# Opening of a hybrid decoder trunk: constant products on TensorE ahead of the first transposes, another order of the first weight loads, and a row load on another queue

## The chip, the core and the metric

The kernel runs on one core of one Trainium2 chip. The core has TensorE (matrix products and transposes into PSUM; its weight loads stand in the profile as PEld), VectorE (DVE), ScalarE (ACT), GpSimd (POOL) and SyncE (SP), which here only issues DMAs. ScalarE and GpSimd issue DMAs too, each on a queue of its own. The metric is the device time of one execution in microseconds; the kernel before and the kernel after are compared by the medians of their runs.

## The reference

One layer over 1024 rows of 1024 channels. A condition vector c makes a shift, a scale and a gate by a product with a 1024 x 3072 matrix; x is normalised, scaled and shifted to h; h goes through one combined input projection; two linear-attention branches run on the projections; they are merged, projected, added to x and normalised. The change lies in the first steps:

```python
c_act = jax.nn.silu(c)
mod = c_act @ ada_w[l] + ada_b[l]
shift, scale, gate = jnp.split(mod, 3, axis=-1)
h = rms_norm(x, norm_w[l]) * (1.0 + scale[:, None, :]) + shift[:, None, :]
proj = h @ w_in[l]
hq, hf, hi, hz, gq, gk, gv, gz, ga, mg = jnp.split(proj, IN_OFFSETS, axis=-1)
```

All inputs are f32. What follows behind the projection (the two attention branches, the gates, the output projection, the final norm) is the same before and after.

## The kernel before

**Numbers.** Products are made in the fp32r form. Each f32 operand is split in two: ScalarE rounds it to a high part (`split`, line 196) and VectorE subtracts that to get the rest, the low part (line 197). A product then is three: high by high, high by low, low by high.

**The opening**, up to `order.close()`, computes h for the first 512 rows and, while h is being made, the first 768 columns of the projection (six blocks of 128, `NG = 6`), for those 512 rows. h is made transposed, in eight tiles d = 0 to 7 of 128 channels. For each d four 128 x 128 blocks of x are transposed on TensorE (`turn_x`, line 219) into a PSUM tile, which ScalarE copies out (`copy_x`, line 224); `make_h` scales and shifts it on ScalarE by that tile's modulation (line 233) and splits it. Then `products(d, ns)` (line 352) adds the 18 products of this d, six for each of the three kinds in `ns`: 0 needs the high parts alone, 1 the low part of h, 2 the low part of the weights.

**Modulation blocks.** Shift and scale come in five blocks, `blocks = [(0, 1), (1, 2), (3, 2), (5, 2), (7, 1)]`, each (first d, number of d). `load_mod(bi)` (line 251) fetches a block's columns: four DMAs of 256 KB for a block of one d, eight for a block of two. `add_mod` (lines 265 and 267, VectorE) sums the first half of the 1024 rows, weighted by c; `mm_mod` (line 277, TensorE) sums the second half as four small f32 matmuls; `end_mod` adds the two (line 283, VectorE), sums over the partitions on TensorE (line 287, the "column sums") and adds the bias (lines 290 and 292).

**Weight tiles.** `load_wg(k)` (line 315) fetches the 768 weight columns of rows 128k to 128k + 127, 384 KB. Tiles 0 to 2 and 5 to 7 share three places, so tile 5, 6 or 7 can be loaded only when tile 0, 1 or 2 has been split. `prep_wg(k)` splits one: two roundings on ScalarE, two subtractions on VectorE.

**Order.** In the opening the order on TensorE, ScalarE and VectorE is that of the program text (`manual_schedule`). DMAs go out in the order of the text on the engine that issues them. Nearly all loads are SyncE's: c, four tiles of x (512 KB each), then block 0, weight tile 0, tiles 1 and 2, block 1, tiles 3 and 4, block 2, and later tiles 5 and 6, block 3, tile 7, block 4 and the second half of x. ScalarE's queue loads `rows_a` (ada_b and norm_w, 24 rows that `vec_rows` transposes on TensorE at line 154); GpSimd loads `rows_b` and the small gate weights. A square, a root, a reciprocal and a product per x tile (lines 203 to 210) normalise x ahead of the transposes.

In the text, behind `load_mod` and `load_wg`, come the squares and scales of x, `vec_rows(rows_a)`, the transposes of d = 0, the sums of block 0, and then a loop over the blocks: make h for this block's d, split the next block's weight tiles, sum the next block's modulation, and between these steps the products. `products` of a d stand around `mm_mod` and `end_mod` of the next block, so that TensorE has work while VectorE sums.

Behind `order.close()` the framework's scheduler sets the order of the instructions on the engines, by times that it models, within the data's dependences. The rest of the kernel (line 541 and on: projections, attention, merging, the products of line 1343, the output stage of line 1520) is ordered so.

Of the kernel before, what the change touches and what calls it, by code (L numbers as in the profile page):

```python
# [9 lines left out]
F32 = mybir.dt.float32  # L10
# [73 lines left out]
def hybrid_trunk_kernel(  # L84
# [6 lines left out]
    nc = tc.nc  # L91
# [17 lines left out]
    def mtile():  # L109
        cnt[0] += 1  # L110
        return ps_m.tile([P, 512], F32, tag="m", name=f"pm{cnt[0]}")

    sc_ps = ps_s.tile([P, T], F32, name="sc_ps")


    ident = cp.tile([P, P], F32, name="ident")
    make_identity(nc, ident)
    ones = cp.tile([P, P], F32, name="ones")
# [11 lines left out]
    rows_c = cp.tile([8, P], F32, name="rows_c")  # L130
    rows_a = cp.tile([24, P], F32, name="rows_a")
# [3 lines left out]
    def row_load(eng, dst, src):  # L135
        eng.dma_start(dst, src.rearrange("(r p) -> r p", p=P))

    def load_x(t):
        b = S.get([D])
        nc.sync.dma_start(b, x2[t * P:(t + 1) * P, :])  # L140
        return b

    row_load(nc.sync, rows_c, c[0])
    x_t = [load_x(t) for t in range(4)]
    row_load(nc.scalar, rows_a[0:16, :], ada_b[0, 0:2 * D])
    row_load(nc.scalar, rows_a[16:24, :], norm_w[0])
    row_load(nc.gpsimd, rows_b[0:8, :], lb_logits[0])
    row_load(nc.gpsimd, rows_b[8:16, :], hgrn_norm_w[0])
    row_load(nc.gpsimd, rows_b[16:20, :], alpha_b[0])
# [2 lines left out]
    def vec_rows(rows, n, at):  # L152
        pv = mtile()
        i = nc.tensor.transpose(pv[:, 0:n], rows, ident[0:n, 0:n])
        nc.vector.tensor_copy(vec[:, at:at + n], pv[:, 0:n])
        return i
# [34 lines left out]
    def split(src, hi=None, lo=None):  # L191

        if hi is None:
            hi = S.get(list(src.shape[1:]), F32R)
            lo = S.get(list(src.shape[1:]), F32R)
        nc.scalar.copy(hi, src)  # L196
        nc.vector.tensor_sub(lo, src, hi.bitcast(F32))  # L197
        return hi, lo
# [8 lines left out]
    def scale_x(t, xt):  # L207
        r = rsx[:, t:t + 1]
        nc.vector.reciprocal(r, r)
        nc.vector.tensor_scalar_mul(xt, xt, r)  # L210

    turned = {}

    def turn_x(half, xs, d):
        if d % 2 == 0:
            hT[half, d // 2] = S.get([2, 512])
        turned[half, d] = mtile()
        for i in range(4):
            nc.tensor.transpose(turned[half, d][:, i * P:(i + 1) * P], xs[i][:, d * P:(d + 1) * P], ident)
        if d == KT - 1:  # L220
            S.free(*xs)

    def copy_x(half, d):
        nc.scalar.copy(hT[half, d // 2][:, d % 2, :], turned.pop((half, d)))

    def transpose_x(half, xs, d):
        turn_x(half, xs, d)
        copy_x(half, d)
# [14 lines left out]
    def load_mod(bi):  # L243
        d0, nd = blocks[bi]
        kq = 4 // nd
        mods[bi] = []
        for kk in range(KT // kq):
            b = S.get([kq, 2, nd * P])
            for half in range(2):
                c0 = half * D + d0 * P  # L250
                nc.sync.dma_start(b[:, :, half, :], ada_w[0, kk * kq * P:(kk + 1) * kq * P, c0:c0 + nd * P].rearrange(
                    "(k p) f -> p k f", p=P))
            mods[bi].append(b)

    def mod_acc(bi):
        nd = blocks[bi][1]
        return scT_f[:, bi % 2 * 512:bi % 2 * 512 + 2 * nd * P].rearrange("p (a f) -> p a f", a=2)
# [13 lines left out]
    def mm_mod(bi):  # L271
        kq = 4 // blocks[bi][1]
        w = 2 * blocks[bi][1] * P
        mod_ps[bi] = mtile()
        for j in range(4):
            k = 4 + j
            nc.tensor.matmul(mod_ps[bi][32 * j:32 * j + 32, 0:w], cs32[:, k, :],
                             mods[bi][k // kq][:, k % kq].rearrange("p a f -> p (a f)"), start=True, stop=True)

    def end_mod(bi):  # L280
        d0, nd = blocks[bi]
        acc = mod_acc(bi)
        nc.vector.tensor_add(acc, acc, mod_ps.pop(bi)[:, 0:2 * nd * P].rearrange("p (a f) -> p a f", a=2))
        pm = mtile()
        for half in range(2):
            for i in range(nd):
                nc.tensor.matmul(pm[:, half * nd + i:half * nd + i + 1], acc[:, half, i * P:(i + 1) * P], one_t,
                                 start=True, stop=True)
        S.free(*mods.pop(bi))
        nc.vector.tensor_add(modv[:, :, d0:d0 + nd], pm[:, 0:2 * nd].rearrange("p (a b) -> p a b", a=2),  # L290
                             vec[:, R_SH:R_SH + 16].rearrange("p (a b) -> p a b", a=2)[:, :, d0:d0 + nd])
        nc.vector.scalar_tensor_tensor(amul[:, d0:d0 + nd], modv[:, 1, d0:d0 + nd], 1.0,
                                       vec[:, R_NW + d0:R_NW + d0 + nd], ALU.add, ALU.mult)
# [3 lines left out]
    wa_hi = [S.get([2, 512], F32R) for _ in range(4)]  # L297
    wa_lo = [S.get([2, 512], F32R) for _ in range(4)]
    wb_hi = [S.get([4, 256], F32R) for _ in range(2)]
    wb_lo = [S.get([4, 256], F32R) for _ in range(2)]  # L300
# [7 lines left out]
    raws = {}  # L308

    def load_wg(k):  # L310
        if k in (3, 4):
            raws[k] = S.get([T])
        else:
            raws[k] = xb_f[:, (k % 5 % 3) * 768:(k % 5 % 3) * 768 + 768]
        nc.sync.dma_start(raws[k][:, 0:NG * P], w_in[0, k * P:(k + 1) * P, C_GQ:C_GQ + NG * P])

    def prep_wg(k):
        raw = raws.pop(k)
        split(raw[:, 0:512], wa_hi[k // 2][:, k % 2, :], wa_lo[k // 2][:, k % 2, :])
        split(raw[:, 512:768], wb_hi[k // 4][:, k % 4, :], wb_lo[k // 4][:, k % 4, :])  # L320
        if k in (3, 4):
            S.free(raw)

    g_state = {}
    wga = cp.tile([P, KT, 16], F32, name="wga")
# [24 lines left out]
    def product(half, d, f, n):  # L350
        a, b = ((0, h_hi), (0, h_lo), (1, h_hi))[n]
        nc.tensor.matmul(accs[f], wg(a, d, f), b[d][:, half * 512:half * 512 + 512],  # L352
                         start=(d == 0 and n == 0), stop=(d == KT - 1 and n == 2))

    def products(d, ns):
        for n in ns:
            for f in range(NG):
                product(0, d, f, n)

    load_mod(0)  # L360
    load_wg(0)
    load_wg(1)
    load_wg(2)
    load_mod(1)
    load_wg(3)
    load_wg(4)
    load_mod(2)
# [1 line left out]
        square_x(i, x_t[i])  # L369
        scale_x(i, x_t[i])  # L370
    vec_rows(rows_a, 24, R_SH)
    transpose_x(0, x_t, 0)
    add_mod(0)
    mm_mod(0)
    end_mod(0)
    prep_wg(0)
    x_t2 = []
    for bi, (d0, nd) in enumerate(blocks):
        ds = range(d0, d0 + nd)
        more = bi + 1 < len(blocks)  # L380
        nxt = range(blocks[bi + 1][0], sum(blocks[bi + 1])) if more else ()
        for d in ds:
            make_h(0, d)
            if (0, d + 2) in turned:
                copy_x(0, d + 2)
        if not more:
            break
        for d in nxt:
            prep_wg(d)
        add_mod(bi + 1)  # L390
        if nd == 1:
            for d in nxt:
                transpose_x(0, x_t, d)
            products(d0, (0,))
            mm_mod(bi + 1)
            products(d0, (1,))
            end_mod(bi + 1)
            products(d0, (2,))
            turn_x(0, x_t, nxt[-1] + 1)
        else:  # L400
            late = x_t2 if bi == 3 else ()
            for i, xt in enumerate(late[:2]):
                square_x(4 + i, xt)
                scale_x(4 + i, xt)
            products(d0, (0, 1))
            if bi > 1:
                transpose_x(0, x_t, nxt[0])
            for i, xt in enumerate(late[2:]):
                square_x(6 + i, xt)
            mm_mod(bi + 1)  # L410
            products(d0, (2,))
            for d in nxt[1:]:
                transpose_x(0, x_t, d)
            products(d0 + 1, (0,))
            end_mod(bi + 1)
            for i, xt in enumerate(late[2:]):
                scale_x(6 + i, xt)
            products(d0 + 1, (1, 2))
        if bi == 0:
            load_wg(5)  # L420
            load_wg(6)
            load_mod(3)
            load_wg(7)
            load_mod(4)
        elif bi == 1:
            x_t2.extend(load_x(t) for t in range(4, 8))
    products(KT - 1, (0,))
# [119 lines left out]
    class Feat:  # L547

        raws, parts = 1, 2
# [16 lines left out]
    class Vblk:  # L566

        raws, parts = 2, 4
# [41 lines left out]
    class Vblk2:  # L610

        raws, parts = 4, 8
# [400 lines left out]
    class First:  # L1013
        raws, parts = 0, 0
# [435 lines left out]
    for g in BUILT[1:]:  # L1450
        n = GROUPS.index(g)
# [201 lines left out]
    for b in (2, 3):  # L1653
        for p, i, z in ((3, 3, "11"), (6, 1, "21"), (6, 3, "12"), (7, 2, "22")):
            after(b - 1, p, i, lambda b=b, z=z: load_quad(b, z))
            if b == 3:
                p, i = {(3, 3): (7, 2), (6, 1): (7, 3), (6, 3): (4, 2), (7, 2): (4, 3)}[p, i]
# [61 lines left out]
```

## Time and profile before

| What | Value |
|---|---|
| Median of 3 runs | 1216.99 us (1215.41 to 1218.84) |
| Profiled execution, its own time | 1216.46 us |
| Its span, first to last instruction | 1214.8 us |
| Mean granted TensorE clock | 0.998 |
| TensorE busy | 1184.1 us, 97% of the span |
| VectorE, ScalarE, GpSimd busy | 65%, 45%, 10% |
| Moved by DMA | 183.51 MB, mean 151 GB/s |

In the rows of the profile, `PE L352 MATMUL pd<-b,b 128*128 128x512 f32 x4` is four matmuls of line 352 on TensorE, into the PSUM tile pd, with a 128 x 128 stationary and a 128 x 512 moving operand. A timeline row begins with its start and its duration in microseconds; a bracket at its end gives how long the engine stood idle before it and what ended that. The fp32r type of the operands of line 352 stands as f32 there. A row of windows has the stretch, its length, the busy time of PE, PEld, DVE, ACT and POOL, the granted clock, the share of the DMA engines, and GB/s. Rows of DMA issues end with the size of each and the time from issue to landing. Matmuls overlap in the pipeline, so the duration of one is longer than the distance to the next.

### The profile page before, as it was taken

To read this page: it belongs to the slowest core of one execution; us is meant where nothing else is said; L and a number is where in the kernel's file an instruction comes from. 1 tells how busy PE (TensorE), PEld (TensorE's weight loads), DVE (VectorE), ACT (ScalarE), POOL (GpSimd) and SP (SyncE) were. 2 spreads that over 40 slices of the span, in tenths; PEclk is the share of its full clock that TensorE was granted. 3 is DMA by queue.
4 is the path that set the end of the run, shared out by engine and by line. 5 is a ranking of instruction groups with operands and counts; after the bars stand their busy time and mean duration, and the time that the engine had idled before them with its cause. 6 is when DMAs were issued, how large, how long until landed. Compare 5 with 4: busy or idle time off the path is not lost.

```text
span 1214.8 us, 20860 instructions
## 1 busy us (share of the span) xinstructions
PE 1184.1 (97%) x8579; PEld 982.6 (81%) x8579; DVE 790.9 (65%) x1245; ACT 546.9 (45%) x797; POOL 123.8 (10%) x215
## 2 busy tenths in 40 slices
PE   5999999999999999999999999999999999999997
PEld 3777889889798888888887888877778888878886
DVE  4637444774848456877884365794653775988994
ACT  5646732434434244344332324455743544444554
POOL 4100000202111121121110101011220000000000
PEclk9999999999999999999999999999999999999999
DMA  9814000844444267255341112054697746435523
GB/s 320 277 70 139 18 19 19 293 141 161 156 152 149 66 207 249 94 179 169 108 174 47 59 53 70 36 174 158 227 343 277 260 160 208 135 104 173 174 104 122
DMA packets 130961, 183.51 MB, mean 151 GB/s; under 512 B 7467, under 2 KB 97633, under 8 KB 130866
## 3 DMA queue, kind: packets, MB, share of 16 engines
q1 hardware_dynamic: 117250, 136.87, 35.7%
q0 software_dynamic: 13568, 45.31, 9.6%
q8 instruction: 67, 1.10, 0.4%
q14 instruction: 28, 0.23, 0.1%
q10 hardware_dynamic: 48, 0.01, 0.0%
HBM read 132.87 MB, written 49.28 MB: 150 GB/s over the span
## 4 chain that ended last, share of the span: by engine, by line
PE 61%; issue 23%; DVE 3%; ACT 3%; POOL 2%; DMA 1%; POOLq 0%; ACTq 0%; DVEq 0%
PE pd L541 19%; PE pd L1343 9%; PE sc_ps L1343 5%; PE pm L1343 5%; PE pd L1520 3%; PE pd L643 2%; PE pd L644 2%; PE pd L645 2%; PE sc_ps L1520 2%; PE pm L848 1%; PE pd L352 1%; PE pm L829 1%; PE pm L850 1%; PE pm L1520 1%; PE sc_ps L352 1%
## 5 line engine op out<-in xcount | busy, mean ns | idle before, releaser
L541 PE MATMUL pd<-b,b 128*128 128x512 f32 x1632 | 387.4, 394 | 0.0
L541 PEld LDWEIGHTS pd<-b,b 128*128 128x128 f32 x1632 | 302.4, 188 | 64.8 <-issue 1.4
L1343 PE MATMUL pd<-b,b 128*128 128x512 f32 x720 | 173.7, 392 | 4.3 <-ACT b L1414 2.1
L1343 PEld LDWEIGHTS pd<-b,b 128*128 128x128 f32 x720 | 133.7, 188 | 35.7 <-ACT b L1414 3.2
L197 DVE TENSOR_TENSOR b<-b,b 128x1024 fp32r<-128x1024 f32 (+2 forms) x89 | 98.9, 1122 | 83.1 <-ACT b L196 65.4
L196 ACT CAST b<-b 128x1024 fp32r<-128x1024 f32 (+2 forms) x89 | 82.9, 948 | 92.1 <-DVE b L1199 14.6
L1286 DVE TENSOR_TENSOR b<-b,b 128x1024 fp32r<-128x1024 f32 x56 | 68.3, 1224 | 66.9 <-ACT b L1285 52.3
L1285 ACT CAST b<-b 128x1024 fp32r<-128x1024 f32 x56 | 58.3, 1050 | 73.9 <-PE pd L1343 20.6
L1343 PE MATMUL sc_ps<-b,b 128*128 128x512 f32 x324 | 79.4, 391 | 1.0 <-ACT scT L793 1.0
L600 PE MATMUL pd<-b,b 128*128 128x256 f32 x256 | 74.2, 290 | 0.0
L1264 DVE TENSOR_TENSOR b<-b,b 128x1024 fp32r<-128x1024 f32 x48 | 59.2, 1251 | 20.8 <-ACT b L1263 15.1
L602 PE MATMUL pd<-b,b 128*128 128x256 f32 x256 | 72.5, 283 | 0.0
L601 PE MATMUL pd<-b,b 128*128 128x256 f32 x256 | 72.4, 283 | 0.0
L1343 PEld LDWEIGHTS sc_ps<-b,b 128*128 128x128 f32 x324 | 60.3, 188 | 14.6 <-ACT scT L793 1.4
L1343 PE MATMUL pm<-b,b 128*128 128x512 f32 x300 | 72.1, 389 | 0.0
L1263 ACT CAST b<-b 128x1024 fp32r<-128x1024 f32 x48 | 49.9, 1050 | 41.2 <-PE pd L1343 16.0
L1343 PEld LDWEIGHTS pm<-b,b 128*128 128x128 f32 x300 | 56.3, 188 | 11.7
L352 PE MATMUL pd<-b,b 128*128 128x512 f32 x192 | 53.3, 410 | 2.0 <-ACT b L196 0.9
L1201 POOL DMA_DIRECT2D ws<-b x64 | 34.6, 541 | 192.0 <-DVE b L1195 86.5
L735 ACT COPY xb<-b 128x512 f32<-128x512 f32 x48 | 29.4, 620 | 49.4 <-PE sc_ps L715 26.7
L643 PE MATMUL pd<-b,b 128*128 128x512 f32 x128 | 51.3, 401 | 0.0
L644 PE MATMUL pd<-b,b 128*128 128x512 f32 x128 | 50.0, 390 | 0.0
(285 smaller groups left out, 1964.3 us busy)
## 6 DMA issues: line engine op xcount, KB each, us to landing
b<-in_w_in_dram SPq DMA_DIRECT2D x66, 512.0 KB, 4.2
ws<-b POOLq DMA_DIRECT2D x64, 256.0 KB, 3.3
b<-ws SPq DMA_DIRECT2D x32, 512.0 KB, 4.9
b<-in_x_dram SPq DMA_DIRECT2D x16, 512.0 KB, 5.7
b<-in_ada_w_dram SPq DMA_DIRECT2D x32, 256.0 KB, 6.9
b<-in_w_branch_dram SPq DMA_DIRECT2D x16, 512.0 KB, 4.4
b<-h SPq DMA_DIRECT2D x14, 512.0 KB, 4.3
wo<-b POOLq DMA_DIRECT2D x14, 512.0 KB, 5.7
```

Of the source, the lines that this page charges most:

```text
L196: nc.scalar.copy(hi, src)
L197: nc.vector.tensor_sub(lo, src, hi.bitcast(F32))
L352: nc.tensor.matmul(accs[f], wg(a, d, f), b[d][:, half * 512:half * 512 + 512], start=(d == 0 and n == 0), stop=(d == KT - 1 and n == 2))
L541: nc.tensor.matmul(ps[0:w, th * 512:(th + 1) * 512], a[:, k, 0:w], b[:, th * 512:(th + 1) * 512], start=(k == 0 and n == 0), stop=(k == KT ...
L600: nc.tensor.matmul(o, lh, hi[:, k % 4, :], start=(k == 0), stop=False)
L601: nc.tensor.matmul(o, lh, lo[:, k % 4, :], start=False, stop=False)
L602: nc.tensor.matmul(o, ll, hi[:, k % 4, :], start=False, stop=(k == KT - 1))
L643: nc.tensor.matmul(o, lh, hi[:, k % 2, :], start=(k == 0), stop=False)
L644: nc.tensor.matmul(o, lh, lo[:, k % 2, :], start=False, stop=False)
L1286: nc.vector.tensor_sub(lo, t, hi.bitcast(F32))
L1343: nc.tensor.matmul(o, a[:, sl], c, start=(p in (1, 5) and kt == 0 and n == 0), stop=(kt == 3 and n == 2), skip_group_check=True)
L1520: nc.tensor.matmul(o, a, b, start=(p in (1, 5) and kt == 0 and n == 0), stop=(kt == 3 and n == 2), skip_group_check=True)
```

## The change

Six edits, all in the opening.

- c is loaded by ScalarE's queue instead of SyncE's, and norm_w by GpSimd's instead of ScalarE's.
- `keep_busy(n)` multiplies two constant 128 x 128 f32 tiles (ones and the identity) n times, into columns of `sc_ps` that the first products overwrite later. Seven stand ahead of the transposes of d = 0; one, three, one and two stand behind the first to the fourth of these transposes; one stands behind `mm_mod(0)`; two stand ahead of the first products.
- Block 1 of the modulation is loaded ahead of weight tiles 1 and 2.
- The split of a weight tile is cut in two functions, `prep_hi` (ScalarE) and `prep_lo` (VectorE).
- Tiles 1 and 2 are no longer split ahead of block 1's sum. Tile 1 is rounded behind that sum, and its subtraction and the split of tile 2 stand between the two h tiles of block 1.
- The loads of tile 6, block 3, tile 7 and block 4 stand behind that place, since tiles 6 and 7 take the places of tiles 1 and 2.

```diff
-    row_load(nc.sync, rows_c, c[0])
+    row_load(nc.scalar, rows_c, c[0])
     x_t = [load_x(t) for t in range(4)]
     row_load(nc.scalar, rows_a[0:16, :], ada_b[0, 0:2 * D])
-    row_load(nc.scalar, rows_a[16:24, :], norm_w[0])
+    row_load(nc.gpsimd, rows_a[16:24, :], norm_w[0])
...
+    def keep_busy(n):
+        for _ in range(n):
+            nc.tensor.matmul(sc_ps[:, 512:640], ones, ident, start=True, stop=True)
+
-    def turn_x(half, xs, d):
+    def turn_x(half, xs, d, gaps=(0, 0, 0, 0)):
...
             nc.tensor.transpose(turned[half, d][:, i * P:(i + 1) * P], xs[i][:, d * P:(d + 1) * P], ident)
+            keep_busy(gaps[i])
...
+    def wg_parts(k):
+        return ((raws[k][:, 0:512], wa_hi[k // 2][:, k % 2, :], wa_lo[k // 2][:, k % 2, :]),
+                (raws[k][:, 512:768], wb_hi[k // 4][:, k % 4, :], wb_lo[k // 4][:, k % 4, :]))
+
+    def prep_hi(k):
+        for raw, hi, _ in wg_parts(k):
+            nc.scalar.copy(hi, raw)
+
+    def prep_lo(k):
+        for raw, hi, lo in wg_parts(k):
+            nc.vector.tensor_sub(lo, raw, hi.bitcast(F32))
         raw = raws.pop(k)
...
     load_mod(0)
     load_wg(0)
+    load_mod(1)
     load_wg(1)
     load_wg(2)
-    load_mod(1)
     load_wg(3)
...
     vec_rows(rows_a, 24, R_SH)
-    transpose_x(0, x_t, 0)
+    keep_busy(7)
+    turn_x(0, x_t, 0, (1, 3, 1, 2))
+    copy_x(0, 0)
     add_mod(0)
     mm_mod(0)
+    keep_busy(1)
     end_mod(0)
     prep_wg(0)
...
             make_h(0, d)
             if (0, d + 2) in turned:
                 copy_x(0, d + 2)
+            if bi == 1 and d == 1:
+                prep_lo(1)
+                prep_wg(2)
+                load_wg(6)
+                load_mod(3)
+                load_wg(7)
+                load_mod(4)
...
-        for d in nxt:
-            prep_wg(d)
+        if bi:
+            for d in nxt:
+                prep_wg(d)
         add_mod(bi + 1)
         if nd == 1:
             for d in nxt:
                 transpose_x(0, x_t, d)
+            keep_busy(2)
             products(d0, (0,))
             mm_mod(bi + 1)
             products(d0, (1,))
             end_mod(bi + 1)
+            prep_hi(1)
             products(d0, (2,))
             turn_x(0, x_t, nxt[-1] + 1)
...
         if bi == 0:
             load_wg(5)
-            load_wg(6)
-            load_mod(3)
-            load_wg(7)
-            load_mod(4)
```

More of the change, by code (lines that the diff above doesn't have):

```diff
@@ L315, in load_wg, with prep_wg @@
         nc.sync.dma_start(raws[k][:, 0:NG * P], w_in[0, k * P:(k + 1) * P, C_GQ:C_GQ + NG * P])
-    def prep_wg(k):
+    def wg_parts(k):
[7 more added lines that the diff above has]
+            nc.vector.tensor_sub(lo, raw, hi.bitcast(F32))
         raw = raws.pop(k)
-        split(raw[:, 0:512], wa_hi[k // 2][:, k % 2, :], wa_lo[k // 2][:, k % 2, :])
-        split(raw[:, 512:768], wb_hi[k // 4][:, k % 4, :], wb_lo[k // 4][:, k % 4, :])
         if k in (3, 4):
             S.free(raw)
+    def prep_wg(k):
+        prep_hi(k)
+        prep_lo(k)
     g_state = {}
```

## The prediction

> **What bounds the kernel now.** First the page, for the engine that is full and for the load on the DMA queues over the span:
>
> ```profile
> span 1214.8 us, 20860 instructions
> ...
> PE 1184.1 (97%) x8579; PEld 982.6 (81%) x8579; DVE 790.9 (65%) x1245; ACT 546.9 (45%) x797; POOL 123.8 (10%) x215
> ...
> DMA  9814000844444267255341112054697746435523
> ```
>
> TensorE carries 97% of the span, so only time in which TensorE stands still, or runs slowly, can be won. Where that is, the view by windows tells, cut at 24.45 us:
>
> ```profile
> 0.00:24.45 24.45, 11.17 (x40) 5.88 (x40) 13.18 (x30) 14.10 (x27) 14.41 (x56) 1.00 0.96 311
> 24.45:1206.90 1182.45, 1172.98 (x8541) 976.70 (x8539) 775.37 (x1212) 530.46 (x766) 109.41 (x159) 1.00 0.45 148
> ```
>
> Behind 24.45 us TensorE is idle for 1182.45 - 1172.98 = 9.5 us in all, 0.8%. Whatever starts that dense stretch earlier ends the kernel earlier, about one for one. Ahead of it 13.3 us are idle, but the DMA engines are 96% busy there. So the opening is a race between loads and the first matmuls. The timeline of TensorE there (start, duration, and in brackets the idle time before and what ended it):
>
> ```profile
> 7.34 0.48 PE L219 MATMUL pm<-ident,b 128*128 128x128 f32 x1 [3.99 <-DVE b L210]
> ...
> 14.47 1.08 PE L277 MATMUL pm<-b,cs 128*32 128x256 f32 x8 [0.88 <-DVE scT L267]
> 16.17 0.99 PE L287 MATMUL pm<-ones,scT 128*128 128x1 f32 x4 [0.62 <-DVE scT L283]
> 17.02 1.95 PE L219 MATMUL pm<-ident,b 128*128 128x128 f32 x8
> 19.17 2.07 PE L352 MATMUL pd<-b,b 128*128 128x512 f32 x4 [0.20 <-ACT b L196]
> ...
> 23.47 1.05 PE L277 MATMUL pm<-b,cs 128*32 128x512 f32 x4 [0.39 <-DMA b<-in_ada_w_dram]
> ...
> 24.45 1.21 PE L352 MATMUL pd<-b,b 128*128 128x512 f32 x4
> ...
> 28.24 0.60 PE L219 MATMUL pm<-ident,b 128*128 128x128 f32 x4
> 28.92 1.20 PE L352 MATMUL pd<-b,b 128*128 128x512 f32 x4
> ...
> 31.86 1.06 PE L277 MATMUL pm<-b,cs 128*32 128x512 f32 x8
> 32.86 1.20 PE L352 MATMUL pd<-b,b 128*128 128x512 f32 x4
> ...
> 37.13 1.02 PE L287 MATMUL pm<-ones,scT 128*128 128x1 f32 x8 [0.79 <-DVE scT L283]
> ```
>
> Two things are to be seen. Four products take 2.07 us at 19.17 and 1.21 us at 24.45, so TensorE runs at about half speed until about 24 us, though the page's granted clock says 1.00 throughout. And the second block's sum (23.47) waits for a load. From 28.92 on only one wait is left in the opening: 0.79 us for VectorE at 37.13.
>
> **The change, part by part.** The loads first:
>
> ```profile
> 0.81 0.41 SPq L136 DMA_DIRECT2D rows_c<-in_c_dram  x1
> 1.27 1.77 SPq L140 DMA_DIRECT2D b<-in_x_dram  x4
> ...
> 25.38 0.37 SPq L251 DMA_DIRECT2D b<-in_ada_w_dram  x1
> 26.19 1.08 SPq L315 DMA_DIRECT2D xb<-in_w_in_dram  x2
> ```
>
> *c by ScalarE's queue*: SyncE's stream starts with x, 1.27 - 0.81 = 0.46 us earlier. With the DMA engines full, every later landing moves by the same 0.46. c itself goes first on a queue that started at the same 0.8 us, so it lands as before.
>
> *norm_w by GpSimd*: GpSimd's first load is the nearest row.
>
> ```profile
> 1.94 0.68 POOL L136 DMA_DIRECT2D rows_b<-in_hgrn_lb_logits_dram  x1
> ...
> rows_b<-in_hgrn_lb_logits_dram POOLq DMA_DIRECT2D x1, 4.0 KB, 5.5
> ```
>
> norm_w takes its place and lands at 1.94 + 5.5 = 7.4 us. The transpose of rows_a waits for it, and on TensorE everything stands behind that transpose: the seven constant products and the transposes of x. The four row loads and the 64 KB load for the gate behind it move by 0.5 to 0.7 us; they are read behind the first half's products, so nothing.
>
> *Constant products*: 7 + 1 + 3 + 1 + 2 = 14 stand ahead of the first modulation sum, one behind it, two ahead of the first products. None is in the trace. A 128-wide f32 pass costs 1.95/8 = 0.24 us at 17.02 and 0.60/4 = 0.15 at 28.24 with the pipeline's end in it, about 0.21 and 0.11 without; the f32 sums show two passes per matmul (x8 for four). I take 0.43 slow and 0.22 fast for one. The ends are nothing (all in idle time) and 14 x 0.43 = 6.0 us. From 7.7 us, with four transposes of 0.21, the slow line ends at 14.55. The sum needs TensorE at 14.47 - 0.46 = 14.01, when its last load lands. If the clock rises at 12.5 the line ends at 13.5 and costs nothing. The one and the two others lie in the waits of 0.62 and 0.20 us and what the faster transposes leave.
>
> What a fast clock is worth is read from the fifth block's rows, the same shapes:
>
> ```profile
> 55.34 0.64 PE L277 MATMUL pm<-b,cs 128*32 128x256 f32 x8
> ...
> 58.77 0.50 PE L287 MATMUL pm<-ones,scT 128*128 128x1 f32 x4
> ```
>
> The first sum saves 1.08 - 0.64 = 0.44, its column sums 0.99 - 0.50 = 0.49. Both are on the chain load, sum, VectorE, column sums, ScalarE, first product. With 0.46 from the queue the first product starts 1.39 earlier, at 17.8. VectorE's own part of that sum follows at 13.45 + 1.53 - 0.46 = 14.5, just ahead of TensorE's 14.65.
>
> Is the clock fast by then? From 16.17 to 23.1 TensorE had work with pauses of 0.2 us at most, eight transposes in it, and was still slow at 23.47; it turned fast some 4 to 5 us after its products began at 19.17. Counted from 7.7 us that gives the 12.5 used above. [...] I take the rise ahead of 14, because ordinary products fill 6.0 of the line's 6.85 us.
>
> *Second modulation block ahead of two weight tiles*: two tiles of 384 KB pass behind it. At the rate of this stretch,
>
> ```profile
> 15.00:20.00 5.00, 4.18 (x22) 3.16 (x15) 2.54 (x7) 3.25 (x7) 0.40 (x3) 1.00 1.08 356
> ```
>
> they take 0.786 MB / 356 GB/s = 2.2 us. The wait at 23.47 ends at 23.47 - 0.46 - 2.2 = 20.8, and the products behind it start at 21.4 instead of 24.45. VectorE no longer splits the two tiles first; its rows:
>
> ```profile
> 17.47 1.03 DVE L197 TENSOR_TENSOR b<-xb,b 128x512 fp32r<-128x512 f32 x2
> ...
> 19.15 0.69 DVE L197 TENSOR_TENSOR b<-b,b 128x512 fp32r<-128x512 f32 x1 [0.65 <-ACT b L196]
> ...
> 22.15 2.33 DVE L267 SCALAR_TENSOR_TENSOR scT<-b,cs,scT 128x512 f32<-128x512 f32 x3
> ...
> 28.90 0.69 DVE L197 TENSOR_TENSOR b<-b,b 128x512 fp32r<-128x512 f32 x1 [1.60 <-ACT b L196]
> 30.86 2.57 DVE L197 TENSOR_TENSOR b<-b,b 128x512 fp32r<-128x512 f32 x5 [1.27 <-ACT b L196]
> ...
> 36.30 0.69 DVE L283 TENSOR_TENSOR scT<-scT,pm 128x512 f32<-128x512 f32 x1
> ```
>
> It finishes h's remainder at 19.15 - 1.39 + 0.69 = 18.45 and the sum at about 21.3, ahead of its use. So the block at 28.92 starts 3.05 us earlier, at 25.87. The first delayed tile lands about 22 us and is rounded on ScalarE in time.
>
> Now the part that gives back. *The splits moved*: four subtractions (2 x 1.03 = 2.06 us) and two roundings go between the two h tiles of the second block. On ScalarE,
>
> ```profile
> 15.34 0.92 ACT L196 CAST b<-xb 128x512 fp32r<-128x512 f32 x2 [1.13 <-DMA xb<-in_w_in_dram]
> ...
> 27.40 0.82 ACT L233 ACTIVATE b<-b,modv,amul 128x512 f32<-128x512 f32 x1 [5.67 <-DVE amul L292]
> ...
> 29.36 0.82 ACT L233 ACTIVATE b<-b,modv,amul 128x512 f32<-128x512 f32 x1
> ```
>
> the second h starts at 29.36 - 3.05 + 0.92 = 27.23, and VectorE's stretch of 30.86 starts 1.5 later, at 28.73 (VectorE is free at 25.85 + 0.69 + 2.06 = 28.6). The end of the third block's sum, 36.30 - 30.86 = 5.44 behind it, comes at 34.2, the column sums of 37.13 at 35.0: 2.1 us earlier, not 3.05.
>
> The loads set nearly the same limit. The third block's last load:
>
> ```profile
> b<-in_ada_w_dram SPq DMA_DIRECT2D x1, 256.0 KB, 5.9
> ```
>
> issued at 25.38 it lands at 31.3; the bytes ahead of it are unchanged, so now 30.85. TensorE gets to that sum at 31.86 - 3.05 = 28.8 and waits 2 us, where before it came 0.6 after the load. The sum ends at 31.5; the work up to the column sums takes 36.18 - 32.86 = 3.3 us as before (36.18 is where TensorE ran dry: 37.13 less the wait and the 0.15 to issue), so 34.85 at the earliest. Both limits give 35.0, and 2.3 us is the most that the opening can give.
>
> *Loads moved behind the splits*: SyncE blocks at the second tile of the row at 26.19 until VectorE has read the old one, 25.85 + 0.69 + 1.03 = 27.6, instead of issuing at 26.5. Fourth block, eighth tile, fifth block and x's second half queue behind it. Eight loads in flight, landing some 0.75 us apart, cover 1.1 us. Uncovered, the fourth block's last load would land near 41.7, still ahead of its use at 44.1 - 2.1 = 42.0. Taken as nothing; 0 to 0.3 us.
>
> **The sum**: 0.46 + 0.93 for the first products, 1.66 more for the second block, -0.95 given back: 2.1 us. The profiled execution took 1216.46 us (span 1214.8 and 1.7 around it), 0.5 below the median 1216.99. 1216.46 - 2.1 = 1214.4.
>
> **The rivals.** *The clock stays slow.* The line ends at 14.55, the first sum at 15.63, and three more slow dummies put the first products at 19.65 instead of 19.17. The load order still gives 0.45 by 24 us, and VectorE's 2.06 us of splits take it back: the column sums come at 37.6, and the time is 1216.9. For it: the slow rows up to 23.47. Against: the dummies are ordinary products, back to back.
>
> *The order behind the opening, better.* Only the opening is ordered by hand; behind it the scheduler places instructions by its own modelled times, which the change shifts. This row shows a small transpose placed between products of another line:
>
> ```profile
> 97.29 0.23 PE L154 MATMUL pm<-ident,rows_b 22*128 22x22 f32 x1
> ```
>
> TensorE's largest waits there:
>
> ```profile
> PE pd L1343 <- ACT b L1414: 2.1, 2, 1.8
> PE pd L1343 <- DVE b L953: 1.5, 1, 1.5
> PE sc_ps L1343 <- ACT scT L793: 1.0, 1, 1.0
> ```
>
> Half of these 4.6 us gone on top of 2.1 gives 1212.1.
>
> *The same, worse: the end on the other side.* Place: the products of line 1343, where operands split by ScalarE and VectorE come just in time. Price: up to 1.8 us for each wait of that kind. It decides from 2.1 + 3.65 = 5.75 us of new waits, four of them at 1.8: 1214.4 + 7.2 = 1221.6. Against: 9.5 idle us in 1182 is little, and most of the order hangs on data.
>
> **How the numbers follow.** 0.3% is 3.65 us, about what a measurement of this kernel can tell from no change. The forecast (1214.4; own range 1213.9 to 1216) has 0.50, the slow clock 0.13: both within. The better order has 0.25, the worse 0.12. So 0.25 faster, 0.63 same, 0.12 slower. The range leaves out the worse order and the lower edge of the better one: 1211.5 to 1218.
>
> **What would show it.** Products at 17.8 and at half duration there; the second block's sum waiting for its load near 20.8; TensorE waiting some 2 us for a load near 29 to 31, where it did not wait; column sums of the third block near 35.0; and behind 40 us the same waits. Wrong, if products are still slow after 20 us, if norm_w lands well after 7.4, or if TensorE's idle time behind 40 us differs from before by more than 1.5 us.

## The result, and the profile after

The changed kernel takes 1218.34 us (median of 22 runs) against 1216.80 of the kernel before (22 runs): ratio 1.0017, 95% interval 1.0009 to 1.0025. It is slower by 1.5 us, where 2.1 us less were forecast, and lies just above the range of 1211.5 to 1218. The profiled execution took 1217.89 us.

First the opening, on TensorE's timeline of the changed kernel (columns as in the prediction):

```profile
8.44 0.30 PE L154 MATMUL pm<-ident,rows_a 24*128 24x24 f32 x1 [5.24 <-DMA rows_a<-in_norm_w_dram]
8.67 3.36 PE L216 MATMUL sc_ps<-ident,ones 128*128 128x128 f32 x14
...
12.45 0.83 PE L216 MATMUL sc_ps<-ident,ones 128*128 128x128 f32 x6
...
14.35 0.64 PE L282 MATMUL pm<-b,cs 128*32 128x256 f32 x8 [0.18 <-POOL mask L531]
...
15.62 0.58 PE L292 MATMUL pm<-ones,scT 128*128 128x1 f32 x4 [0.21 <-DVE scT L288]
...
18.20 1.20 PE L369 MATMUL pd<-b,b 128*128 128x512 f32 x4 [0.62 <-ACT b L196]
...
21.37 1.05 PE L282 MATMUL pm<-b,cs 128*32 128x512 f32 x4 [0.48 <-DMA b<-in_ada_w_dram]
...
26.81 1.19 PE L369 MATMUL pd<-b,b 128*128 128x512 f32 x4
...
30.33 1.05 PE L282 MATMUL pm<-b,cs 128*32 128x512 f32 x4 [0.50 <-DMA b<-in_ada_w_dram]
31.75 1.05 PE L282 MATMUL pm<-b,cs 128*32 128x512 f32 x4 [0.36 <-DMA b<-in_ada_w_dram]
...
36.24 1.02 PE L292 MATMUL pm<-ones,scT 128*128 128x1 f32 x8
```

The opening does what it was to do. Fourteen dummy passes take 3.36 us slow (0.21 apart), six take 0.83 fast, so the clock rises near 12.2 us; the record of the granted clock begins at 12.20. The products at 18.20 take 1.20 us, not 2.07; the second block's products start at 26.81 instead of 28.92; the third block's column sums at 36.24 instead of 37.13. At the end of the first half's products (107.52 us against 108.68) TensorE is 1.17 us ahead. Yet its last matmul ends at 1208.58 us, before at 1206.85. The waits of TensorE behind 40 us, in the view of waits (total us, times, longest), the changed kernel first, then the kernel before:

```profile
PE pd L1369 <- ACT b L1440: 3.3, 2, 3.0
PE pd L1369 <- DVE b L979: 1.5, 1, 1.5
PE sc_ps L741 <- DVE tot L744: 1.3, 1, 1.3
```

```profile
PE sc_ps L715 <- DVE tot L718: 0.7, 1, 0.7
```

(The rows for the other two stand in the prediction: 1.8 and 1.5 us at longest.) Two waits have grown, by 0.65 us at 313 us and by 1.18 us at 893 us. What the clock does at the longer one shows in the view by windows over 892.84 to 896.25 us, changed kernel and kernel before:

```profile
892.84:896.25 3.41, 2.87 (x7) 2.29 (x8) 0.00 (x0) 0.49 (x1) 0.54 (x1) 0.50 0.99 363
```

```profile
892.84:896.25 3.41, 3.38 (x15) 2.81 (x16) 0.00 (x0) 0.55 (x1) 0.54 (x1) 1.00 1.01 365
```

PEclk is 0.50 for these 3.41 us, and 7 matmuls fall into them where 15 did. The ledger, as the start of the same instruction in both traces: 1.17 us ahead at 107, 0.87 at 253, 0.22 at 313, 0.10 behind at 621, 0.56 ahead again at 860, 0.51 behind at 893, and 1.82 behind at 896 us, where the slow stretch ends. From there to the end it changes little (1.73 behind at the last matmul).

### The profile page after: what moved, and what is told of

Its sections match the earlier page's. It is cut to its first block, busy times and chain, and to the rows that moved or that the text cites. A ratio compares the mean times of both kernels' runs of the same rounds, so it can differ in the third digit from the quotient of the medians.

```text
span 1216.2 us, 20925 instructions
## 1 busy us (share of the span) xinstructions
PE 1188.0 (98%) x8613; PEld 987.4 (81%) x8613; DVE 790.9 (65%) x1245; ACT 547.3 (45%) x797; POOL 123.1 (10%) x216
## 4 chain that ended last, share of the span: by engine, by line
PE 57%; issue 24%; DVE 5%; ACT 3%; POOL 3%; DMA 2%; POOLq 0%; DVEq 0%; ACTq 0%
PE pd L567 16%; PE pd L1369 9%; PE sc_ps L1369 5%; PE pm L1369 5%; PE pd L1546 3%; PE pd L669 2%; PE pd L671 2%; PE pd L670 2%; PE sc_ps L1546 2%; PE pd L369 1%; PE pm L874 1%; PE pm L1546 1%; PE pm L855 1%; PE pm L876 1%; DMA ws<-b 1%
## 5 line engine op out<-in xcount | busy, mean ns | idle before, releaser
L197 DVE TENSOR_TENSOR b<-b,b 128x1024 fp32r<-128x1024 f32 (+1 forms) x85 | 97.0, 1147 | 83.2 <-ACT b L196 64.6
L196 ACT CAST b<-b 128x1024 fp32r<-128x1024 f32 (+1 forms) x85 | 81.4, 969 | 95.0 <-DVE b L1225 14.5
L761 ACT COPY xb<-b 128x512 f32<-128x512 f32 x48 | 29.4, 620 | 50.7 <-PE sc_ps L741 27.4
```

## The experiments

The order of the instructions behind the opening is the same in both kernels, on every engine, so the two rivals of another order fell without a run. The first theory was a *late wait*: the stages behind wait for landings that do not move with TensorE, and a long one (3.0 us in this profile) goes with 3.41 us at half clock. In all that follows, times are medians in us, and ratios are against the kernel before on the same chip, with their 95% interval.

### The wait itself, and a delay

> The changed kernel once more, as it is. Theory of the late wait: the opening gains 1.2 us (the work at 107 us starts earlier than before), then TensorE's wait for the sigmoid of an odd gate tile near 893 us is again about 3 us long (1.82 before), and the products of the last stage behind it run at half speed for about 4 us; the end is 1 to 2 us later than before. Rival (chance landing): the wait at 893 comes out anywhere between 1.8 and 3 us without pattern, no slow products follow it, and the kernel is within 0.5 us of before.

1217.56 us, ratio 1.0011 (1.0002 to 1.0019). The work at 107 us starts at 107.14, the waits are 1.31 us at 313 and 2.45 us at 893, and the clock is halved from 892.96 to 896.38: as expected, with a somewhat shorter wait.

```diff
 def put_gate1(d, half, ap, summed):
+    if not summed and not Q.open:
+        S.free_list.rotate(-1)
     g = ap if summed else Q.get()
```

> The changed kernel, in which the free list is turned by one place before an odd gate tile takes its slot, so that the sigmoid near 893 us writes a slot that no store is reading. Theory of the late wait: the 3.0 us wait and the slow products behind it (about 1.3 us) go, the time falls by about 4 us to 1214 us, and is about 1 us under the kernel before with the same edit, which is the opening's gain. Rival (another operand is late next): TensorE waits as long at the same place for something else, and the time stays at 1218. Rival (cost in the opening): the time falls by the same 1.8 us as in the kernel before, and stays 1 to 2 us above it.

> The kernel before with the same turn of the free list. Theory of the late wait: its 1.82 us wait near 893 goes, no products were slow behind it, so the time falls by about 1.8 us to 1215 us. Rival (another operand is late next): no change, 1216.8 us.

After: 1218.97, ratio 1.0020 (1.0007 to 1.0033). Before: 1216.66, ratio 1.0001 (0.9993 to 1.0010). The wait near 893 is gone, and another stands behind it in the changed kernel (waits from 885 to 912 us):

```profile
PE pd L1369 <- ACT b L1311: 1.7, 1, 1.7
PE sc_ps L1369 <- DVE b L1312: 0.5, 1, 0.5
PE pd L1369 <- DVE b L1312: 0.5, 1, 0.5
```

The split of a weight pair is late next, as the rival had it. Taking the wait away at that place earns nothing.

```diff
-    def end_mod(bi):
+    def end_mod(bi, pad=0):
...
+        for _ in range(pad):
+            nc.tensor.matmul(pm[:, 256:384], ones, ident, start=True, stop=True)
...
-            end_mod(bi + 1)
+            end_mod(bi + 1, 9 if bi == 3 else 0)
```

> The kernel before with 9 multiplications of constant tiles (18 matrix instructions 0.111 us apart, 2.0 us in all) behind the column sums of the last modulation block, in the dense part of the opening. Theory of the late wait (what waits for landings far behind does not follow TensorE): the work at 108.68 us starts 2.0 us later, the wait near 893 us falls from 1.82 us to near zero, and the end is 0 to 0.8 us later. Rival (all is paced by TensorE): every wait keeps its length and the end is 2.0 us later.

1218.51, ratio 1.0013 (1.0005 to 1.0022). The work at 107 us is 2.0 us later, the wait at 893 still 1.57 us, the end 1.7 us later by the medians, as the rival had it. The profile alone does not settle it: there the delay has shrunk to 1.4 us by 621 us, and a stretch at half clock from 646.18 us, behind no wait, adds 1.6; and the 18 instructions also lengthen the code, which matters below. Clearer is a gain that goes through: in the two profiles of the changed kernel without dummies (next part), TensorE is 2.3 and 1.6 us ahead of the kernel before at 107 us, and 2.2 and 1.7 us at its last matmul. So the first theory does not explain where the gain went.

### The parts

> The changed kernel with the two row loads back on their old queues (the condition's row on SyncE's, the norm weight on ScalarE's); the dummies and the new order of loads stay. Theory of the late wait (the opening's gain of about 1.2 us at 107 us is used up by waits for landings near 313, 812 and 893 us, and a wait over 2 us near 893 us then halves TensorE's clock for one stretch of 3.41 us, 1.3 us more): the wait near 893 us stays over 2 us, the mean granted clock of the timed runs stays near 0.9963 (0.9976 before), and the time is 1217.5 to 1218.5 us. Rival (GpSimd's extra load shifts every later transfer of GpSimd to another queue, and that is what makes the gate's store land late): the wait near 893 us is back at 1.8 us, the clock at 0.9976, the time at 1216 us or below.

> The changed kernel without the multiplications of constant tiles; the queues and the new order of loads stay. Theory of the late wait: the clock rises near 20 us as before, the first products start 0.5 to 0.9 us later than in the changed kernel (18.2 us), the work at 107 us starts 0.3 to 0.9 us later than its 107.3, and the end does not follow: 1217 to 1218.5 us, with the wait near 893 us at 2 us or more. Rival (the dummies cost by themselves): 1216 us or less. Rival (the dummies earn what the opening gains, and the end follows): 0.5 to 0.9 us above the changed kernel.

> The kernel before with the multiplications of constant tiles and the two new queues; the order of loads and splits stays as before. Theory of the late wait: half of the opening's gain (first products 0.9 us earlier, but the second block's sum still waits for its last load near 23.4 us, so the work at 107 us starts 0 to 0.4 us earlier than before); the wait near 893 us is 1.8 to 2.2 us, clock and time are near those of the kernel before, 1216.3 to 1217.3 us. Rival (the dummies or the queues make the loss): 1218 us, with the clock at 0.9963.

> The kernel before once more, for a second profile. Theory of the late wait: its wait near 893 us is again below 2 us, no stretch of halved clock follows it, and the work at 107 us starts within 0.5 us of 108.68. Rival (chance landing): the wait is anywhere between 1.5 and 3 us.

| kernel | median | ratio | wait at 313 | wait at 893 |
|---|---|---|---|---|
| changed, old queues | 1218.92 | 1.0024 (1.0015 to 1.0034) | 1.38 | 2.90 |
| changed, no dummies | 1214.50 | 0.9990 (0.9980 to 0.9999) | 0.56 | 1.53 |
| before, dummies and queues | 1219.84 | 1.0030 (1.0020 to 1.0041) | 1.61 | 2.83 |
| before | 1216.02 | 1.0000 (0.9990 to 1.0010) | under 0.3 | 1.68 |

The dummies make the loss, with the old queues as with the new, and with the old order of loads too; the late wait's expectations of the second and third kernel missed. They are over at 17.6 us and lengthen two waits at 313 and 893 us. Both waits hang on a store by GpSimd: at 313 VectorE's sums of weights wait for the landing of the store of one branch's output (yg), whose buffer they write next (waits of VectorE from 300 to 313 us, changed kernel):

```profile
DVE b L1222 <- DMA yg<-b: 4.3, 1, 4.3
```

and at 893 ScalarE's sigmoid waits for the landing of an earlier gate half (4.81 us in the kernel before, 5.55 in the changed one). The view of DMAs, restricted to 887 to 892.6 us, lists what the DMA engines carry there (queue, kind: packets, MB, share of 16 engines), the kernel before first, then the changed one:

```profile
q0 software_dynamic: 414, 1.50, 66.2%
q1 hardware_dynamic: 1319, 0.65, 39.8%
```

```profile
q0 software_dynamic: 445, 1.61, 71.3%
q1 hardware_dynamic: 1147, 0.58, 35.8%
q8 instruction: 1, 0.02, 1.2%
```

One kind of packet is new in this stretch, which the page calls instruction. The changed kernel's page has 67 of them on queue q8, 1.10 MB, 16 KB each, over 8613 weight loads and as many matmuls: one for about 128 pairs of TensorE. From this count they are taken for blocks of TensorE's code, fetched over DMA while it runs. With 34 pairs more in the opening the fetches come earlier in the program: by the trace's packets the first stands at 27.4 us instead of 35.2, the one at 306.2 us in the kernel before at 302.2, and the one at 897.4 at 890.0; the two stores are under way there from 300.6 to 305.6 and from 887.1 to 892.6 us. TensorE itself shows no stall for its code: behind 40 us no wait of it over 0.2 us ends without a releaser on another engine. The stores beside the code take longer: 4.9 us for yg, where it was 4.1, and 5.6 for the gate half, where it was 4.8 (medians by the view of DMAs, GpSimd's issues at 300 to 302 and 886.5 to 889.6 us).

### The place of the code

The edit, with 34, 12, 26, 94 or 128 for n; the transposes write PSUM columns that nothing reads:

```diff
+    for _ in range(n):
+        nc.tensor.transpose(sc_ps[0:8, 512:520], ident[0:8, 0:8], ident[0:8, 0:8])
     vec_rows(rows_a, 24, R_SH)
```

> The changed kernel without its multiplications of constant tiles, but with 34 small transposes (8x8, of a constant tile) on TensorE in the idle time ahead of the rows' transposes at 8.4 us, so that TensorE's instruction stream is as long as in the changed kernel. Theory of the code block (every 128 pairs of weight load and matmul TensorE fetches a block of 16 KB of its instructions by DMA; the 34 pairs of the dummies move these fetches to about 27, 302 and 890 us, where they lie among transfers that TensorE waits for): the fetches move from 39.1, 303.6 and 895.7 us to about 27, 302 and 888 us, the wait near 312 us grows to over 1 us and the one near 891 us from 1.5 to over 2.3 us, and the time is 1216.5 to 1218.5 us against 1214.5 without the transposes. Rival (the dummies' warm clock or their work is what costs): 1214.5 us as without them.

> The kernel before with the same 34 small transposes and nothing else. Theory of the code block: the fetches near 306 and 897 us move to about 302 and 890 us, the wait near 313 us grows from 0 to 0.7 to over 1.2 us, the wait near 893 us from 1.7 to over 2.4 us, TensorE's clock is halved for a stretch of 3.41 us behind it, and the time is 1218 to 1219.5 us. Rival: no change, 1216.5 us.

> As the run before, with 12 small transposes. Theory of the code block: the fetches move by a third as much, to about 36, 302 and 893 us: the wait near 312 us grows to about 1 us, the one near 891 us stays at 1.5 us, and the time is 1214.5 to 1215.5 us. Rival (the dummies' warm clock or their work is what costs): 1214.5 us and both waits as without them.

> The changed kernel with 26 small transposes more (60 pairs more than before in all). Theory of the code block: the fetches move on to about 22, 299 and 884 us, ahead of the transfers that TensorE waits for near 313 and 893 us; the wait near 893 us falls from 2.4 to 3.0 us to below 2 us, the halved clock behind it goes, and the time falls to 1215.5 to 1216.8 us although TensorE has more to do. Rival (the dummies' warm clock or their work is what costs): 1218 us or more.

The transposes cost nothing where they stand: in the kernel before, 34 of them take 0.99 us of idle time (TensorE's timeline):

```profile
2.56 0.99 PE L372 MATMUL sc_ps<-ident 8*8 8x8 f32 x34
3.42 0.27 PE L154 MATMUL pm<-ident,rows_a 24*128 24x24 f32 x1
```

But the kernel before, with them, took 1218.30, ratio 1.0018 (1.0004 to 1.0031), as much as the whole change. These are its waits from 300 to 320 and from 885 to 905 us, its code block from 887 to 892.6, and its gate store (KB, us to landing):

```profile
PE sc_ps L717 <- DVE tot L720: 1.6, 1, 1.6
PE pd L1345 <- ACT b L1416: 2.5, 1, 2.5
```

```profile
q8 instruction: 1, 0.02, 1.1%
...
gate<-b POOLq DMA_DIRECT2D x1, 256.0 KB, 5.5
```

The two waits are not all of this profile's loss. By the start of the same instruction in both kernels, TensorE loses 0.9 us near 313 and 0.6 near 893, but 1.6 in a stretch at half clock that follows no wait; the one that was expected behind 893 did not come:

```profile
645.94:649.36 3.42, 3.42 (x10) 2.64 (x9) 1.05 (x1) 0.35 (x1) 0.00 (x0) 0.50 0.33 85
```

The changed kernel without dummies but with 34 transposes: 1218.99, ratio 1.0027 (1.0016 to 1.0038), waits of 1.25 and 2.24 us, fetches at 301.2 and 890.2, and half clock both at 644.39 and at 893.56. Its clock rises only at 19.75 us, so no early rise is needed for the loss, only the length of the code.

With 12 the fetch near 305 lies behind the store and the wait at 893 is 1.60 us, but the time is 1218.05, ratio 1.0016 (1.0003 to 1.0029): the expectation missed, and its profile, of 1215.6 us, does not show what the slower runs lost. With 26 more in the changed kernel the wait at 893 fell to 1.70 us as expected, but the wait at 313 stayed at 1.46, waits of 1.30 us at 253 and 0.80 us at 339 came up, and the time was 1219.88, ratio 1.0031 (1.0019 to 1.0043): that expectation missed too. The two stores do not explain these two kernels; that the fetches matter at other places as well is a guess. The test that does not depend on which is a whole block:

> The kernel before with 128 small transposes (a whole block of TensorE's code, 3.3 us at 0.026 us each, in the idle time ahead of 7.3 us). Theory of the code block: the fetches come back to their places without padding (near 35, 306 and 897 us), the waits near 313 and 893 us to 0 to 0.7 us and 1.7 us, the time to 1216 to 1217 us. Rival (added instructions cost as such, wherever the fetches fall): 1218 us or more, as with 34 of them.

> The changed kernel with 94 small transposes more, so that with its own 34 pairs a whole block is added. Theory of the code block: the fetches come to the places that they have without the dummies (near 37, 304 and 896 us), the wait near 893 us falls from 2.4 to 3.0 us to 1.6 us without a halved clock behind it, and the time is 1214 to 1215.5 us. Rival (added instructions, or the warm clock, cost as such): 1218 us or more.

> The changed kernel without its multiplications of constant tiles, with 128 small transposes. Theory of the code block: as without the transposes, 1214 to 1215.5 us, with waits of 0.6 us near 311 and 1.5 us near 891 us. Rival (added instructions cost as such): 1218 us or more, as with 12 or 34 of them.

> The changed kernel without its multiplications of constant tiles, a second time. Theory of the code block: 1214 to 1215.5 us again, 0.1 to 0.2% under the kernel before, with a mean granted clock near 0.9978. Rival (the first time was chance): within 0.05% of the kernel before or above it.

> The changed kernel with 94 small transposes, a second time. Theory of the code block: 1214.5 to 1216 us again, below the kernel before, the fetch near 897 us and the wait near 893 us below 2 us. Rival (the first time was chance): 1217 us or more.

| kernel | pairs added | median | ratio | wait at 893 |
|---|---|---|---|---|
| before | 128 | 1216.98 | 1.0006 (0.9996 to 1.0016) | 1.65 |
| changed | 34 + 94 | 1215.77 | 0.9992 (0.9984 to 1.0001) | 1.65 |
| changed, second time | 34 + 94 | 1214.84 | 0.9985 (0.9975 to 0.9995) | 1.49 |
| changed, no dummies | 128 | 1216.59 | 1.0004 (0.9994 to 1.0015) | 1.36 |
| changed, no dummies, second time | 0 | 1216.21 | 1.0003 (0.9992 to 1.0015) | 1.29 |

More instructions, and less time: 94 transposes on top of the changed kernel take 0.25% off it (1.0017 to 0.9992, and 1.0011 to 0.9985), some 3 us. Repeats of one kernel differ by up to 0.13%, so a single row of 0.1% says little; these two pairs differ by twice that. Two expectations missed: the changed kernel without dummies was to be faster than the kernel before again, and with 128 transposes too, and came out level with it both times. So the gain of its first measurement (0.9990) was at least in part chance. The first profile with 94 transposes has a half-clock stretch too, at 811.70 us behind a wait of 2.40. The second of these runs, by its page's first line, its waits, its gate store, and the 94 transposes that do it:

```profile
span 1213.1 us, 21113 instructions
```

```profile
PE sc_ps L743 <- DVE tot L746: 0.3, 1, 0.3
PE pd L1371 <- ACT b L1442: 1.5, 1, 1.5
```

```profile
gate<-b POOLq DMA_DIRECT2D x1, 256.0 KB, 4.0
```

```profile
2.42 2.49 PE L389 MATMUL sc_ps<-ident 8*8 8x8 f32 x94
```

Over the 20 profiles of all kernels the two stores sort themselves by whether a code block starts while they are under way (time from issue to landing, us):

```text
                    no code block      a code block
store before 313    3.72 to 4.29 (12)  4.88 to 5.25 (7)
gate half at 887    3.94 to 4.81 (13)  4.80 to 5.55 (7)
```

(One more, with 26 transposes, took 5.10 us though its block was fetched ahead of it, at 298.3; the sorting does not explain that one. All seven with a block are kernels with exactly 34 pairs more.) A code block's packet takes 1.05 us by the trace's packets (median of the 67 in the kernel before), a 4 KB packet of these stores 0.16; the stores land 1.2 and 1.4 us later by the medians. How the one makes the other late was not shown.

### The order alone

```diff
-    row_load(nc.scalar, rows_c, c[0])
+    row_load(nc.sync, rows_c, c[0])
...
-    row_load(nc.gpsimd, rows_a[16:24, :], norm_w[0])
+    row_load(nc.scalar, rows_a[16:24, :], norm_w[0])
```

(from the changed kernel without dummies)

> The kernel before with the new order of loads and splits alone: no multiplications of constant tiles, both row loads on their old queues. Theory of the code block (no pair is added, so the fetches stay in place): the second block's sum moves up by 2 us, the work at 107 us starts 0.8 to 2 us earlier than 108.68, the waits near 313 and 893 us are as before, and the time is 0.5 to 1.5 us under the kernel before. Rival (the order earns nothing without the queue): within 0.3 us of the kernel before.

1216.03, ratio 0.9992 (0.9981 to 1.0003): unclear. In its profile the products behind the second block's sum start 1.2 us earlier (23.26), but the third block's column sums wait 1.73 us for VectorE and start at 37.16 us, no earlier than before, and the work at 107 us starts at 108.4. The order alone moves the opening's end by nothing in that profile; nor does it in the changed kernel with old queues (108.73), whose clock rose only at 22.81 us; the first dummies there ran at 3.6 us, and the transposes came late. With the new queues that work starts at 107.1 to 107.7 in six profiles of the changed kernel, with and without added transposes or the turned list, against 108.0 to 108.7 in five of the kernel before. Without dummies, with queues and order alone, it starts at 106.4, 107.1, 107.2, 108.2 and 109.0: 0.8 us ahead in the mean, but scattered. So the dummies add little that these profiles can show.

## Why the prediction was wrong, point by point

**The clock** came out: a rise at 12.2 us (12.5 forecast), the first sum 0.64 us and its column sums 0.58 long, products at full speed from 18.20. The slow-clock rival fell. The instant was partly luck. In the kernel before, the record of the granted clock begins at 22.02 us, 2.9 us behind the first products, and the sum at 23.47 was not slow: its matmuls take as long as those at 31.86. So the 4 to 5 us that gave 12.5 were too long, and the line began later than taken. In the seven profiles with dummies and the new queues the rise came between 10.5 and 14.3 us. Of the four transposes only the first, at 11.82, lay ahead of the rise at 12.20, so this profile does not show whether transposes delay it.

**The queue** was mis-sized. The term was 0.46 us for every landing. The first sum began at 14.35, not at 14.01: the last load of its block landed at 14.22. The dummies' line was no earlier: norm_w landed at 8.40 instead of 7.4, the line started at 8.44 instead of 7.7, and its last pass ended at 14.17. The first products started 0.97 earlier instead of 1.39. Between profiles of the same opening they moved from 16.66 to 18.7 us, more than the term itself.

**The second block** was right in kind: its wait ended at 21.37 instead of 20.8, its products came 2.11 us earlier instead of 3.05. Part of that was in the sum: the work between that wait and the products lasts 0.98 us in both kernels, so a wait that ends at 20.8 puts them at 21.8, not at 21.4.

**The third block** was right in kind, and dearer: TensorE waits for its loads at 30.33 and 31.75, as forecast, but the last lands near 31.6, not 30.85. The column sums gained 0.89 us, not 2.1. The sum of 2.1 us was 1.17 in this profile and about 1.0 over the six and five profiles above.

**The step that failed** is the cost of the constant products: "The ends are nothing (all in idle time)", and with it "behind 40 us the same waits". Their time was indeed nothing. Their 34 pairs of instructions, a quarter of a code block (34 of about 128), moved the code fetches, two of them onto stores that TensorE waits for. In the profiled execution that goes with 0.65 us more of waiting at 313, 1.18 at 893, and 1.31 us of halved clock behind that, 3.1 us in all. That the length of the code makes the loss is shown by the runs with transposes; that it does so through these two stores fits the profiles of 34 pairs, and not those of 12 and 60. With a whole block added the same change is 0.08 and 0.15% faster than before, 1.0 and 1.8 us (the first not clear of nothing): the direction that was forecast, at half to nearly all of the size.

**The rival on the other side** named the right place, the products behind 800 us whose operands come just in time, and a like price. Its mechanism, a new order of the instructions, was not the one.

## What to carry to other kernels

In this kernel added instructions cost the shift of the code as well as their own time: 12 to 60 pairs more went with a result worse by 0.1 to 0.3% (in the changed kernel 34 of them shifted the code fetches at 306 and 897 us by 4.0 and 7.4 us), where the whole edit was to gain less than 0.2%. Before such an edit is blamed or praised, measure it once more with idle-time instructions that fill its addition up to a whole code block (here 128 pairs of TensorE), and look in the DMA view for instruction packets inside the landings that the largest waits hang on. Here a gain measured against a kernel of another code length included this: 0.9992 and 0.9985 with the block filled up, 1.0017 and 1.0011 without.

## What had not been expected of the hardware

**Half-clock stretches in mid-run.** The clock's record in the changed kernel shows 880.639 us at full speed, 3.413 us at half, 317.440 at full: 258, 1 and 93 times 3.4133. They come with TensorE's long waits (2.24, 2.40, 2.45, 2.90 and 3.00 us in the profiles above), but not each time (the waits of 2.5 us near 893 in the kernel before with 34 transposes and of 2.83 with dummies and queues had none). Cut into stretches of 3.4133 us from its first rise on, the changed kernel's record has 2.46 us of TensorE's idle time in the stretch just ahead of the slow one, and at most 1.09 in any other up to the last matmul; the kernel before, cut the same way, has at most 1.40 and no slow stretch. These two give no threshold, and why one wait brings a slow stretch and another of like length none was not shown. Four profiles show one near 645 us without any wait (at 644.39, 645.94 and 646.18 in three of them), behind eight f32 matmuls with a ones tile, some 0.5 us apart. The kernel before and the changed kernel have the same eight from 640.92 and 641.00 us on and no slow stretch behind them, so this kind stays open.

**They go with about half of the spread between runs.** Each timed run lists its mean granted clock. Over 388 timed runs of all kernels the time goes with it by 0.9 us per 0.001 (correlation -0.70 within kernels, so about half of the variance); one stretch of 3.413 us at half is 0.0014 of the span. The mean also counts half clock behind the last matmul, 0.0010 in the changed kernel's profile, which costs nothing. The mean is 0.9963 for the changed kernel (34 runs), 0.9977 for the kernel before (162), 0.9979 with the 94 transposes (22). By the slope the 0.0014 between the first two go with 1.3 us, most of the difference of 1.5 us; a correlation does not say which is the cause.

**What stays open**: why 12 added pairs cost 0.16%, with both stores clear of the code, and 60 cost 0.31%; and whether the dummies earn anything once the code is in place (0.9992 and 0.9985 with them, 0.9990, 1.0003 and, with 128 transposes, 1.0004 without).
